# Two token-major projections joined into one 512 columns wide, in a two-layer hybrid decoder kernel

## The chip, the core and the metric

The kernel runs on one core of a Trainium2 chip. A core has TensorE (matrix products, PE in the profile, with its weight loads listed apart as PEld), VectorE (DVE), ScalarE (ACT), GpSimd (POOL) and a queue that only starts transfers (SP). Each of them works through its own list of instructions in order, and semaphores hold an instruction back until what it needs has been done elsewhere. The metric is the device time of one execution in microseconds (us), lower is better. Three runs of the kernel before took 1769.89, 1771.38 and 1771.6 us; their median is 1771.38.

## The reference

The computation is a decoder trunk of two equal layers on 512 tokens of width 1024. Cut to what matters here, a layer is:

```python
h = rms_norm(x, ln1)
u = h @ w_in                       # one projection; its columns are split among all branches
(fq, fk, fv, ff, gq, gk, gv, glr, gr, rq, rk, rv, rg, z, xbc, dt, gates) = split_cols(u, IN_SPLITS)
y_a = forgetting_attention(fq, fk, fv, ff + fox_bf, ...)      # softmax attention with decay
o_b = gla_chunked(gq, gk, gv, log_a)                          # gated linear attention
o_c = retention_chunked(rotary(rq), rotary(rk), rv, log_gamma)
o_d = ssd_chunked(...)                                        # state-space scan
x = x + (sum over the branches of sigmoid(gate_b) * (y_b @ w_up_b)) @ w_out
x = x + swiglu(rms_norm(x, ln2), w_ffn_in, w_ffn_out)
```

`fv` and `rv` are the values of the forgetting attention and of the retention: 512 tokens by 256 columns each.

## The kernel before, in words

**Products.** To keep float32 accuracy, every operand of a large product is split into a high and a low part in a reduced-precision format (`xh` and `xl` for the normed input, `wh` and `wl` for weights). One logical product is then three matrix instructions into the same PSUM bank, issued by `mm3` (line 164): high by high, low of the stationary side by high, high by low of the moving side. All of them go through line 162, so the profile gives nearly all of TensorE's work that one line, and the tiles tell the work apart. A name like `mm<-xh,wl` reads: result in an `mm` bank, moving operand `xh`, stationary operand `wl`.

**Weights.** All weights come as 300 slabs of eight 128 by 128 blocks, in the order in which `block` (line 236) asks for them. For each slab there is one transfer (`wr`), a cast on ACT to `wh` (line 176) and a subtraction on DVE to `wl` (line 177). Two slabs of raw weights and three of split weights fit in SBUF.

**Projections.** Most column groups of `w_in` are projected feature-major: the weight block is stationary, 512 tokens move, eight steps of the inner dimension give 24 instructions into one bank (`proj`). The first four of a layer run together step by step into four `mx` banks (`group`), since at the start weights and inputs are only arriving. The values are needed token-major: there the tokens are stationary (128 at a time, four groups `tb`) and the weight columns move. `tokmajor` (line 469) does this for `rv` and, later, for `fv`: 256 columns move, two groups of tokens share a bank, so one such projection uses two of the four `mm` banks. At its end ACT scales the results of `rv` by the norm (`v`), and for `fv` ACT writes a high part and DVE the low part of a split tile (lines 490 and 491).

**Order of the work.** The four mixers (`ssd`, `gla`, `ret`, `fox`) are chains of small products, exponentials and elementwise work. Each is a Python generator, and at each `yield` the function `drain` lets `pull` emit dense projections from the list `fill`, until their costs (the numbers that stand with them in the list, in us) add up to a budget, `PACE`. What a projection costs over the budget is owed and is taken from the next ones. So the costs in the list set which dense work stands between two steps of a chain. A scheduler then sets the final order of each engine's list, with its own model of time.

In `gla`, the steps that matter here are: cumulated gates by small float32 products (line 784) into two banks `mx`; from each bank an exponential on ACT (line 786), a product on POOL with the queries (line 787), a second exponential and a product on DVE with the keys (line 790), a copy and a subtraction on DVE (lines 793 and 796); then products of those queries and keys, the scores (line 811), after memsets on POOL of parts of the tiles that will take them (line 815).

Of the kernel before, what the change touches and what calls it, by code (L numbers as in the profile page):

```python
# [10 lines left out]
F32 = mybir.dt.float32  # L11
F32R = mybir.dt.float32r
I32 = mybir.dt.int32
AF = mybir.ActivationFunctionType
ALU = mybir.AluOpType
# [3 lines left out]
P = 128  # L19
S = 512  # L20
D = 1024
KD = D // P
NB = S // P
# [3 lines left out]
NH = 4  # L27
# [3 lines left out]
C_FQ, C_FK, C_FV, C_FF = 0, 256, 512, 768  # L31
C_GQ, C_GK, C_GV, C_GLR, C_GR = 772, 1028, 1284, 1540, 1556
C_RQ, C_RK, C_RV, C_RG = 1812, 2068, 2324, 2580
# [92 lines left out]
def trunk(ctx: ExitStack, tc: tile.TileContext, keys, xin, pos, wst, par, ext, cst, out):  # L126
    nc = tc.nc
    V, A, G, T = nc.vector, nc.scalar, nc.gpsimd, nc.tensor
# [5 lines left out]
    vp = ctx.enter_context(tc.tile_pool(name="vp", bufs=2))  # L134
# [7 lines left out]
    def nm(s):  # L142
        uid[0] += 1
        return f"{s}{uid[0]}"

    def TT(dtype=F32):
        return tp.tile([P, S], dtype, tag="t", name=nm("t"))

    def MM():
        return pm.tile([P, S], F32, tag="mm", name=nm("mm"))  # L150
# [10 lines left out]
    def mm(o, l, r, start, stop):  # L161
        T.matmul(o, lhsT=l, rhs=r, start=start, stop=stop, skip_group_check=True)  # L162

    def mm3(o, l, r, start, stop):
        (lh, ll), (rh, rl) = l, r
        mm(o, lh, rh, start, False)
        mm(o, ll, rh, False, False)
        mm(o, lh, rl, False, stop)

    def mm2(o, l, r, start, stop):  # L170
        pairs = [(a, r) for a in l] if isinstance(l, tuple) else [(l, b) for b in r]
# [19 lines left out]
    def act(out, in_, func, **kw):  # L191
        want = {AF.Ln: "natural_log_exp_and_others", AF.Exp: "natural_log_exp_and_others", AF.Silu: "silu_and_others", AF.Sin: "silu_and_others", AF.Sigmoid: "sigmoid_and_others"}.get(func)
        pre = None
        if want and want != seen["set"]:
            pre = A.preload_act_table_set(want)  # L195
            if seen["last"] is not None:
                order(pre, seen["last"])
            seen["set"] = want
            seen["pre"] = pre
        i = A.activation(out=out, in_=in_, func=func, **kw)  # L200
        if want:
            order(i, seen["pre"])
            seen["last"] = i
        return i
# [31 lines left out]
    def block(*key, width=1):  # L236
        n = len(keys)
        if n % SLAB == 0:
            ahead(n // SLAB + AHEAD)
            if n // SLAB:  # L240
                ready[n // SLAB - 1] = None
        for i in range(width):
            keys.append(key[:-1] + (key[-1] + i * P,))
        i = n % SLAB
        hi, lo = ready[n // SLAB]
        sl = slice(i * P, (i + width) * P)
        return hi[:, sl], lo[:, sl]
# [153 lines left out]
    def layer(l, n1):  # L401
# [4 lines left out]
        fill = []  # L406
# [59 lines left out]
                dst[i] = scaled(proj("w_in", l, c, n1, KD), scale)  # L466
            return TILE, go

        def tokmajor(dst, c, stacked=False):
            st = {}  # L470

            def go(half):
                def f():
                    if half == 0:
                        if not stacked:
                            dst.append(vp.tile([P, NB, 256], F32, tag="v", name=nm("v")))
                        st["ps"] = [MM(), MM()]
                    for k in range(4 * half, 4 * half + 4):
                        w = block("w_in", l, k, c, width=2)
                        for tb in range(NB):  # L480
                            ts = slice(tb * P, (tb + 1) * P)
                            o = st["ps"][tb // 2][:, (tb % 2) * 256:(tb % 2) * 256 + 256]
                            mm3(o, (n1.hi[:, k, ts], n1.lo[:, k, ts]), w, k == 0 and tb % 2 == 0, k == KD - 1)
                    if half:
                        for tb in range(NB):
                            v, rt = st["ps"][tb // 2][:, (tb % 2) * 256:(tb % 2) * 256 + 256], n1.rt[:, tb:tb + 1]
                            if stacked:
                                t = TT(F32R).rearrange("p (h s d) -> p h s d", h=NH, s=2)
                                v = v.rearrange("p (h d) -> p h d", h=NH)
                                act(out=t[:, :, 0], in_=v, func=AF.Copy, scale=rt)  # L490
                                V.scalar_tensor_tensor(out=t[:, :, 1], in0=v, scalar=rt, in1=t[:, :, 0].bitcast(F32), op0=ALU.mult, op1=ALU.subtract)
                                dst.append(t)
                            else:
                                act(out=dst[0][:, tb], in_=v, func=AF.Copy, scale=rt)
                return f
            return [(4.1, go(0)), (4.1, go(1))]

        if l == 0:
            rotary()
# [6 lines left out]
        for k in range(KD):  # L506
            w = wide(l, k)
# [629 lines left out]
        fill += silus([C_GR, C_GR + P, C_RG, C_RG + P])  # L1137
        fill += [keep(rq, j, C_RQ + P * j) for j in range(2)] + [keep(rk, j, C_RK + P * j) for j in range(2)]
        drain(ssd(), PACE[0])
        fill += tokmajor(rv, C_RV)  # L1140
        fill += gate_quad(3, 0) + mix(gate_quad(3, 1), up_of(3, 0))
        drain(gla(), PACE[1])
        fill += [keep(fq, j, C_FQ + P * j) for j in range(2)] + [keep(fk, j, C_FK + P * j) for j in range(2)]
        fill += [(0.0, fox_sums)] + tokmajor(fv, C_FV, True) + [(0.0, fox_rows)]
        fill += mix(gate_quad(1, 0), up_of(3, 1)) + mix(gate_quad(1, 1), up_of(1, 0))
        drain(ret(), PACE[2])
        fill += mix(gate_quad(2, 0), up_of(1, 1)) + mix(gate_quad(2, 1), up_of(2, 0)) + mix(gate_quad(0, 0), up_of(2, 1))
# [144 lines left out]
```

## Time and profile before

| | |
|---|---|
| median of three runs | 1771.38 us (1769.89 to 1771.6) |
| profiled execution, its own time | 1771.39 us |
| span of its instructions | 1769.7 us (1.7 us lie around it) |
| TensorE matmuls | busy 1760.0 us, 99% of the span, 8700 instructions |
| TensorE weight loads | busy 1463.6 us, 83%, 8700 instructions |
| VectorE, ScalarE, GpSimd | busy 1041.5, 684.8 and 230.3 us |
| mean granted TensorE clock | 0.999 |

Matmuls are pipelined: a record of one is longer than the distance to the next, so the distance between two starts is what an instruction costs on TensorE, and a busy share of 99% only says that there is hardly a stretch without any. Weight loads run beside the matmuls before them. In a row of the timeline, the first two columns are the start and the length in us, `x4` is the count that was merged into the row, and brackets tell how long the engine had been idle before it and what ended that. In a row of a group, the numbers behind the bar are the busy time in us, the mean length of one in ns and the idle time before them.

### The profile page before, as it was taken

The numbers are of one execution on the slowest core, as the hardware profiler recorded it, in microseconds if no ns is written. First come the engines' busy times: TensorE is split into PE (matmuls) and PEld (weight loads), VectorE is DVE, ScalarE is ACT, GpSimd is POOL, SyncE is SP. The second block draws the span as 40 slices with busy tenths as digits, with TensorE's granted clock in tenths as the row PEclk, the third lists the DMA queues.
The fourth block names the chain that finished last, engine by engine and source line by source line (L and its number), as shares of the span: only waits on it lengthen the run. The fifth ranks groups of instructions, "written<-read, shape, count | busy, mean of one in ns | idle before, by whom it ended". The sixth has DMA issues, their size and how long they took to land.

```text
span 1769.7 us, 21568 instructions
## 1 busy us (share of the span) xinstructions
PE 1760.0 (99%) x8700; PEld 1463.6 (83%) x8700; DVE 1041.5 (59%) x1427; ACT 684.8 (39%) x926; POOL 230.3 (13%) x210
## 2 busy tenths in 40 slices
PE   8999999999999999999999999999999999999999
PEld 7878888888888888888888788888888888888887
DVE  5866675777674443444447676867775644334442
ACT  5424543555443321223324254345554432223221
POOL 2032120022101110011000321201220111001100
PEclk9999999999999999999999999999999999999999
DMA  5322222222232222222323222222222323222222
GB/s 188 108 72 72 73 84 77 91 84 84 93 98 95 96 95 96 96 97 95 107 84 107 72 73 71 84 84 84 95 79 84 103 96 101 98 95 96 95 96 95
DMA packets 46036, 163.31 MB, mean 92 GB/s; under 512 B 5104, under 2 KB 5488, under 8 KB 45936
## 3 DMA queue, kind: packets, MB, share of 16 engines
q1 hardware_dynamic: 45072, 160.45, 27.5%
q10 hardware_dynamic: 864, 1.48, 0.3%
q8 instruction: 68, 1.11, 0.3%
q14 instruction: 32, 0.26, 0.1%
HBM read 159.81 MB, written 2.10 MB: 91 GB/s over the span
## 4 chain that ended last, share of the span: by engine, by line
PE 98%; ACT 0%; DVE 0%; DMA 0%; issue 0%; DVEq 0%; ACTq 0%
PE mm L162 83%; PE mx L162 14%; PE mx L1033 1%; DMA x<-in_x_dram 0%; PE mx L633 0%; DVE xl L355 0%; DVE t L367 0%; ACT xh L200 0%; ACT t L200 0%; PE mx L905 0%; PE mx L825 0%; DVE wl L177 0%; ACT wh L176 0%; ACT L195 0%; PE mx L621 0%
## 5 line engine op out<-in xcount | busy, mean ns | idle before, releaser
L176 ACT CAST wh<-wr 128x1024 fp32r<-128x1024 f32 (+1 forms) x300 | 313.1, 1045 | 737.8 <-PE mm L162 599.5
L162 PE MATMUL mm<-xh,wl 128*128 128x512 f32 x1504 | 589.2, 392 | 0.0
L162 PE MATMUL mm<-xh,wh 128*128 128x512 f32 x1504 | 589.1, 392 | 0.0
L162 PE MATMUL mm<-xl,wh 128*128 128x512 f32 x1504 | 588.1, 391 | 0.0
L177 DVE TENSOR_TENSOR wl<-wr,wh 128x1024 fp32r<-128x1024 f32 (+1 forms) x300 | 409.9, 1366 | 285.6 <-ACT wh L176 284.6
L162 PE MATMUL mm<-t,wh 128*128 128x512 f32 x1152 | 367.5, 390 | 0.0
L162 PEld LDWEIGHTS mm<-xh,wh 128*128 128x128 f32 x1504 | 282.5, 188 | 58.9 <-issue 1.3
L162 PEld LDWEIGHTS mm<-xl,wh 128*128 128x128 f32 x1504 | 282.5, 188 | 58.9 <-issue 1.3
L162 PEld LDWEIGHTS mm<-xh,wl 128*128 128x128 f32 x1504 | 282.6, 188 | 58.5 <-issue 1.1
L162 PEld LDWEIGHTS mm<-t,wh 128*128 128x128 f32 x1152 | 216.4, 188 | 44.7
L162 PE MATMUL mm<-t,wl 128*128 128x512 f32 x576 | 224.8, 390 | 0.0
L1178 POOL TENSOR_TENSOR t<-t,t 128x512 f32<-128x512 f32 x44 | 56.8, 1290 | 538.6 <-DVE t L1176 467.4
L162 PEld LDWEIGHTS mm<-t,wl 128*128 128x128 f32 x576 | 108.2, 188 | 22.0
L176 ACT CAST t<-t 128x512 fp32r<-128x512 f32 x112 | 68.7, 621 | 88.5 <-POOL t L1178 42.0
L177 DVE TENSOR_TENSOR t<-t,t 128x512 fp32r<-128x512 f32 x112 | 78.2, 704 | 29.6 <-ACT t L176 22.9
L1176 DVE TENSOR_TENSOR t<-mm,t 128x512 f32<-128x512 f32 x40 | 27.7, 691 | 115.0 <-PE mm L162 115.0
L200 ACT ACTIVATE t<-t 128x512 f32<-128x512 f32 x121 | 73.7, 628 | 24.2 <-DVE t L1175 14.5
L1126 POOL TENSOR_TENSOR t<-t,t 128x512 f32<-128x512 f32 x32 | 43.6, 1361 | 249.1 <-DVE t L1122 243.7
L162 PE MATMUL mx<-t,t 64*128 64x128 f32 (+6 forms) x576 | 63.8, 290 | 0.0
L1175 DVE TENSOR_TENSOR t<-mm,t 128x512 f32<-128x512 f32 x40 | 27.6, 691 | 61.1 <-PE mm L162 61.1
L162 PEld LDWEIGHTS mx<-t,t 128*128 128x128 f32 (+3 forms) x576 | 50.5, 165 | 14.2 <-issue 8.0
L162 PE MATMUL mx<-xh,wl 128*128 128x512 f32 x128 | 50.7, 400 | 3.0 <-DVE wl L177 3.0
(210 smaller groups left out, 1661.2 us busy)
## 6 DMA issues: line engine op xcount, KB each, us to landing
wr<-in_wst_dram SPq DMA_DIRECT2D x296, 512.0 KB, 3.3
out_dram<-x SPq DMA_DIRECT2D x8, 256.0 KB, 2.4
x<-in_x_dram SPq DMA_DIRECT2D x3, 512.0 KB, 6.3
wr<-in_wst_dram SPq DMA_DIRECT2D x4, 256.0 KB, 5.9
x<-in_x_dram SPq DMA_DIRECT2D x2, 256.0 KB, 5.4
cs<-in_cst_dram ACTq DMA_DIRECT2D x1, 462.0 KB, 5.9
pr<-in_par_dram ACTq DMA_DIRECT2D x2, 167.0 KB, 5.1
posi<-in_pos_dram ACTq DMA_DIRECT2D x1, 256.0 KB, 6.8
```

What stands on the lines that cost most here:

```text
L162: T.matmul(o, lhsT=l, rhs=r, start=start, stop=stop, skip_group_check=True)
L176: A.copy(out=hi, in_=src)
L177: V.tensor_tensor(out=lo, in0=src, in1=hi.bitcast(F32), op=ALU.subtract)
L200: i = A.activation(out=out, in_=in_, func=func, **kw)
L1033: T.transpose(ps[:, W:W + P], zs[qb][:, kb * P:(kb + 1) * P], ident)
L1126: (V if last else G).tensor_tensor(out=merged[d], in0=merged[d], in1=t, op=ALU.add)
L1175: V.tensor_tensor(out=a, in0=pg, in1=n2.r, op=ALU.mult)
L1176: V.tensor_tensor(out=u, in0=pu, in1=n2.r, op=ALU.mult)
L1178: G.tensor_tensor(out=a, in0=a, in1=u, op=ALU.mult)
```

## The change

`tokmajor` now does both projections at once: it asks for the blocks of `rv` and `fv` together (two blocks each), moves 512 columns, and gives each of the four groups of tokens a bank of its own, so that it takes all four `mm` banks. At its end it empties each bank three times: ACT for `rv`, ACT and DVE for `fv`. Its two halves stand in the list at a cost of 7.6 each, at the place where `rv` stood alone at 4.1 each (the fill of `gla`); the place of `fv` in the fill of `ret` is empty. In `mm3` the last two of the three products change places, so that the two which share the stationary high part follow each other. `block` learns to take a tuple of two columns.

```diff
     def mm3(o, l, r, start, stop):
         (lh, ll), (rh, rl) = l, r
         mm(o, lh, rh, start, False)
-        mm(o, ll, rh, False, False)
-        mm(o, lh, rl, False, stop)
+        mm(o, lh, rl, False, False)
+        mm(o, ll, rh, False, stop)
...
         for i in range(width):
-            keys.append(key[:-1] + (key[-1] + i * P,))
+            c = key[-1][i // 2] + i % 2 * P if isinstance(key[-1], tuple) else key[-1] + i * P
+            keys.append(key[:-1] + (c,))
...
-        def tokmajor(dst, c, stacked=False):
-            st = {}
+        def tokmajor():
+            st = []
 
             def go(half):
                 def f():
                     if half == 0:
-                        if not stacked:
-                            dst.append(vp.tile([P, NB, 256], F32, tag="v", name=nm("v")))
-                        st["ps"] = [MM(), MM()]
+                        rv.append(vp.tile([P, NB, 256], F32, tag="v", name=nm("v")))
+                        st.extend(MM() for _ in range(NB))
                     for k in range(4 * half, 4 * half + 4):
-                        w = block("w_in", l, k, c, width=2)
+                        w = block("w_in", l, k, (C_RV, C_FV), width=4)
                         for tb in range(NB):
                             ts = slice(tb * P, (tb + 1) * P)
-                            o = st["ps"][tb // 2][:, (tb % 2) * 256:(tb % 2) * 256 + 256]
-                            mm3(o, (n1.hi[:, k, ts], n1.lo[:, k, ts]), w, k == 0 and tb % 2 == 0, k == KD - 1)
+                            mm3(st[tb], (n1.hi[:, k, ts], n1.lo[:, k, ts]), w, k == 0, k == KD - 1)
                     if half:
                         for tb in range(NB):
-                            v, rt = st["ps"][tb // 2][:, (tb % 2) * 256:(tb % 2) * 256 + 256], n1.rt[:, tb:tb + 1]
-                            if stacked:
-                                t = TT(F32R).rearrange("p (h s d) -> p h s d", h=NH, s=2)
-                                v = v.rearrange("p (h d) -> p h d", h=NH)
-                                act(out=t[:, :, 0], in_=v, func=AF.Copy, scale=rt)
-                                V.scalar_tensor_tensor(out=t[:, :, 1], in0=v, scalar=rt, in1=t[:, :, 0].bitcast(F32), op0=ALU.mult, op1=ALU.subtract)
-                                dst.append(t)
-                            else:
-                                act(out=dst[0][:, tb], in_=v, func=AF.Copy, scale=rt)
+                            rt = n1.rt[:, tb:tb + 1]
+                            t = TT(F32R).rearrange("p (h s d) -> p h s d", h=NH, s=2)
+                            v = st[tb][:, 256:].rearrange("p (h d) -> p h d", h=NH)
+                            act(out=rv[0][:, tb], in_=st[tb][:, :256], func=AF.Copy, scale=rt)
+                            act(out=t[:, :, 0], in_=v, func=AF.Copy, scale=rt)
+                            V.scalar_tensor_tensor(out=t[:, :, 1], in0=v, scalar=rt, in1=t[:, :, 0].bitcast(F32), op0=ALU.mult, op1=ALU.subtract)
+                            fv.append(t)
                 return f
-            return [(4.1, go(0)), (4.1, go(1))]
+            return [(7.6, go(0)), (7.6, go(1))]
...
-        fill += tokmajor(rv, C_RV)
+        fill += tokmajor()
...
-        fill += [(0.0, fox_sums)] + tokmajor(fv, C_FV, True) + [(0.0, fox_rows)]
+        fill += [(0.0, fox_sums), (0.0, fox_rows)]
```

What the built lists show at three places follows; rows stand as the lists have them, and numbers in the names tell buffers apart. Lines of the changed kernel lie three lower in `gla` than those of the profile (784 for 787 and so on).

**The start, third slab of weights.** TensorE, the first `group` of the first layer (`mx12` to `mx15` are its four banks, `wh16` and `wl17` the two parts of the third slab). Before:

```order
L162 MATMUL mx12_149<-xh6_119,wh16_177 128x512 [waits Activation_49]
L162 MATMUL mx13_150<-xh6_119,wh16_177 128x512
L162 MATMUL mx14_151<-xh6_119,wh16_177 128x512
L162 MATMUL mx15_152<-xh6_119,wh16_177 128x512
L162 MATMUL mx12_149<-xh6_119,wl17_178 128x512 [waits DVE_49]
L162 MATMUL mx12_149<-xl7_120,wh16_177 128x512
```

And now:

```order
L162 MATMUL mx12_149<-xh6_119,wh16_177 128x512 [waits Activation_49]
L162 MATMUL mx12_149<-xl7_120,wh16_177 128x512 [waits DVE_49]
L162 MATMUL mx13_150<-xh6_119,wh16_177 128x512
L162 MATMUL mx13_150<-xl7_120,wh16_177 128x512
L162 MATMUL mx14_151<-xh6_119,wh16_177 128x512
L162 MATMUL mx14_151<-xl7_120,wh16_177 128x512
L162 MATMUL mx15_152<-xh6_119,wh16_177 128x512
L162 MATMUL mx15_152<-xl7_120,wh16_177 128x512
L162 MATMUL mx12_149<-xh6_119,wl17_178 128x512 [waits DVE_49]
```

Before, four products stand ahead of the first that needs the low part of the weights; now eight do.

**The end of the joint projection, the start of `gla`.** TensorE, first layer. `mx286` and `mx291` are the two banks of cumulated gates, `mm313` is a dense projection. Before, ahead of the scores:

```order
L162 MATMUL mx286_1627<-cr_99,t276_1504 128x128 [waits DVE_49]
L162 MATMUL mx286_1627<-cr_99,t276_1504 128x128
L162 MATMUL mx291_1645<-cr_99,t276_1504 128x128 x2
L162 MATMUL mm313_1768<-xh6_119,wh307_1719 128x512
L162 MATMUL mm313_1768<-xh6_119,wl308_1720 128x512
```

Some 30 dense products follow in that list before the first of the scores. Now the two banks are `mx288` and `mx293`, `mm281` is the fourth bank of the joint projection, the scores go to `mx308` and `mx309`, and `mm313`, the next dense projection, takes over the bank of the first group of tokens:

```order
L162 MATMUL mx293_1595<-cr_99,t276_1504 128x128 x2
L162 MATMUL mm281_1516<-wl300_1616,xh6_119 128x512
L162 MATMUL mm281_1516<-wh299_1615,xl7_120 128x512
L162 MATMUL mx308_1689<-t125_824,t290_1585 128x128 [waits DVE_49,PE_49,Pool_49]
L162 MATMUL mx309_1690<-t125_824,t290_1585 128x128 [waits PE_49]
L162 MATMUL mx308_1689<-t125_824,t290_1585 128x128
L162 MATMUL mx309_1690<-t125_824,t290_1585 128x128
L162 MATMUL mx308_1689<-t125_824,t290_1585 128x128
L162 MATMUL mx309_1690<-t125_824,t290_1585 128x128
L162 MATMUL mx308_1689<-t125_824,t290_1585 128x128
L162 MATMUL mx309_1690<-t125_824,t290_1585 128x128
L162 MATMUL mm313_1710<-xh6_119,wh302_1645 128x512 [waits DVE_49]
```

Two dense products are left between the cumulated gates and the scores. The four products into `mx288` and two more into `mx293` stand directly ahead of this piece. The second layer has the same sequence.

**DVE and POOL at that place, now.** On DVE, `t290` and `t295` are the products with the keys, `t304` is the low part of `fv` of the first group of tokens, read from the bank that `mm313` waits for:

```order
L787 TENSOR_TENSOR t290_1585<-t152_941,t290_1585 128x512 [waits Activation_49]
L790 COPY bl291_1588<-mx288_1577 128x8 [waits PE_49]
L793 TENSOR_TENSOR t289_1582<-bl291_1588,mx288_1577 128x512 [waits DVE_49,Pool_49]
L787 TENSOR_TENSOR t295_1603<-t166_1000,t295_1603 128x512 [waits Activation_49]
L790 COPY bl296_1606<-mx293_1595 128x8 [waits PE_49]
L490 SCALAR_TENSOR_TENSOR t304_1673<-mm278_1513,rt40_317,t304_1673 128x4x64 [waits Activation_49]
```

Before, no reading of a value bank stood among these. On POOL, all four memsets now stand between the two products with the queries, where one stood before:

```order
L784 TENSOR_TENSOR t125_824<-t125_824,t289_1582 128x512 [waits Activation_49]
L812 MEMSET t310_1699 64x4x64 [waits DVE_49]
L812 MEMSET t311_1704 64x4x64 [waits DVE_49]
L812 MEMSET t319_1752 64x4x64 [waits DVE_49]
L812 MEMSET t320_1757 64x4x64 [waits DVE_49]
L784 TENSOR_TENSOR t142_892<-t142_892,t294_1600 128x512 [waits Activation_49]
```

The other three memsets had been issued ahead of the first of these products.

## The prediction

> **What bounds the kernel now.** I read the page first: the busy times and the chain that ended last.
>
> ```profile
> PE 1760.0 (99%) x8700; PEld 1463.6 (83%) x8700; DVE 1041.5 (59%) x1427; ACT 684.8 (39%) x926; POOL 230.3 (13%) x210
> PE 98%; ACT 0%; DVE 0%; DMA 0%; issue 0%; DVEq 0%; ACTq 0%
> ```
>
> TensorE carries the chain from end to end, so the time is the number of its instructions times their distance, plus the few stretches in which it waits. The distance comes from the timeline: ten feature-major products, then fifteen of the projection of `rv`.
>
> ```profile
> 360.68 0.39 PE L162 MATMUL mm<-xl,wh 128*128 128x512 f32 x1
> ...
> 362.95 0.39 PE L162 MATMUL mm<-t,wh 128*128 128x512 f32 x1
> ...
> 171.19 0.28 PE L162 MATMUL mm<-wl,xh 128*128 128x256 f32 x1
> ...
> 172.99 0.28 PE L162 MATMUL mm<-wl,xh 128*128 128x256 f32 x1
> ```
>
> 512 columns take (362.95 - 360.68) / 10 = 0.227 us and 256 columns (172.99 - 171.19) / 15 = 0.120 us. Twice 0.120 less 0.227 leaves 0.013 us: each instruction costs that much whatever its width.
>
> Where TensorE waits, the first 30 us show it: the first `group`, at its third slab of weights.
>
> ```profile
> 20.25 1.07 PE L162 MATMUL mx<-xh,wh 128*128 128x512 f32 x4
> 23.92 0.80 PE L162 MATMUL mx<-xh,wl 128*128 128x512 f32 x1 [2.60 <-DVE wl L177]
> 24.51 0.63 PE L162 MATMUL mx<-xl,wh 128*128 128x512 f32 x1
> ...
> 27.07 0.52 PE L162 MATMUL mx<-xl,wh 128*128 128x512 f32 x1
> 27.43 0.40 PE L162 MATMUL mx<-xh,wh 128*128 128x512 f32 x1
> ...
> 30.15 1.07 PE L162 MATMUL mx<-xh,wh 128*128 128x512 f32 x4
> ```
>
> The same place in windows of 3.4 us; the columns are the busy time of PE, PEld, DVE, ACT and POOL, each with its count, then the granted clock, the DMA share and GB/s.
>
> ```profile
> 20.50:23.92 3.42, 0.82 (x4) 0.35 (x3) 3.42 (x4) 1.05 (x1) 3.30 (x5) 1.00 0.00 0
> 23.92:27.33 3.41, 3.41 (x8) 2.73 (x9) 2.70 (x3) 0.80 (x2) 0.41 (x1) 0.50 0.60 183
> ```
>
> After a window in which TensorE was busy for 0.82 of 3.42 us, it got half the clock for the next 3.41 us, and eight products from 23.92 to 27.43 cost 0.43 us each instead of 0.227. The waits of TensorE and a window over the rest show that nothing of the kind comes later:
>
> ```profile
> PE mx L162 <- DVE wl L177: 3.0, 2, 2.6
> 40.00:1760.00 1720.00, 1720.00 (x8535) 1431.38 (x8534) 1017.64 (x1399) 662.21 (x892) 219.36 (x196) 1.00 0.27 90
> ```
>
> From 40 to 1760 us it is busy without a gap and at full clock.
>
> **The change part by part.** *Half as many instructions, each twice as wide.*
>
> ```profile
> L162 PE MATMUL mm<-wh,xh 128*128 128x256 f32 x128 | 36.4, 284 | 0.0
> L162 PE MATMUL mm<-wh,xl 128*128 128x256 f32 x128 | 36.2, 283 | 0.0
> L162 PE MATMUL mm<-wl,xh 128*128 128x256 f32 x128 | 36.2, 283 | 0.0
> ```
>
> These are 384 instructions on the path, 384 x 0.120 = 46.1 us. They become 192 at 0.227, 43.6 us: **-2.5 us**. The evacuations (eight of `rv`, eight pairs of `fv`) stay the same in number and width.
>
> *The order within mm3.* Over the whole list, 85 neighbours shared a stationary operand before, and 2407 do now: 2322 new pairs. Such a pair exists in the trace, a sum over the partitions whose high and low parts both meet the constant ones (`cr`):
>
> ```profile
> 298.64 0.41 PEld L162 LDWEIGHTS mx<-t,cr 128*128 128x128 f32 x2
> 298.87 0.62 PE L162 MATMUL mx<-t,cr 128*128 128x512 f32 x2
> 299.33 0.40 PE L162 MATMUL mm<-t,wh 128*128 128x512 f32 x1
> ```
>
> Two loads for two products, and (299.33 - 298.87) / 2 = 0.230 us each, against 0.227 where the operand changes. The load is part of each product, it is hidden either way, and its repetition saves nothing. I take **0**; 0.003 us either way, the size of that difference, would be 7 us over 2322 pairs, and I keep that as a bound of low weight. The Trainium skill ("TensorE: Matmul & The Clock Gate", Part 2) says that loading apart from computing lets one load serve many products; the trace shows that this program doesn't do so. What it would give is the third rival.
>
> *The start.* In the third slab, eight products instead of four now stand ahead of the wait for `wl` (the first pair of lists above). The wait itself ends where it did, since DVE comes to that subtraction without a pause and without TensorE:
>
> ```profile
> 19.07 2.44 DVE L355 SCALAR_TENSOR_TENSOR xl<-x,pr,xh 128x512 fp32r<-128x512 f32 x2
> 21.43 1.09 DVE L367 TENSOR_TENSOR t<-t,t 128x512 f32<-128x512 f32 x1
> 22.44 1.42 DVE L177 TENSOR_TENSOR wl<-wr,wh 128x1024 fp32r<-128x1024 f32 x1
> ```
>
> From 23.92 on four products of this step are left instead of eight. If the clock still halves: 4 x 0.43 to 25.64, four of the next twelve to 27.36, eight at 0.227 to 29.18, where 30.15 stands above: **-1.0 us**. If it stays full (TensorE would be busy for about 1.5 us of that window instead of 0.82): 16 x 0.227 to 27.55, -2.6 us. I take -1.0 and keep both ends.
>
> *The start of gla, in each layer.* Here the change adds two waits. Before, a long stretch of dense work lay between the cumulated gates and the scores; now, by the list above, two products do. The chain in between, from the trace of before:
>
> ```profile
> 194.95 1.05 PE L162 MATMUL mx<-cr,t 128*128 128x128 f32 x8
> 195.76 0.48 PE L162 MATMUL mm<-xh,wh 128*128 128x512 f32 x1
> 195.59 2.07 ACT L200 ACTIVATE t<-mx 128x512 f32<-128x512 f32 x4 [0.97 <-PE mx L162]
> 196.27 1.29 POOL L787 TENSOR_TENSOR t<-t,t 128x512 f32<-128x512 f32 x1 [20.71 <-ACT t L200]
> 197.51 0.31 POOL L815 MEMSET t<- 64x256 f32 x1
> 197.78 1.49 POOL L787 TENSOR_TENSOR t<-t,t 128x512 f32<-128x512 f32 x1
> 196.71 1.40 DVE L790 TENSOR_TENSOR t<-t,t 128x512 f32<-128x512 f32 x1 [0.84 <-ACT t L200]
> 198.03 0.15 DVE L793 COPY bl<-mx 128x8 f32<-128x8 f32 x1
> 198.11 1.70 DVE L790 TENSOR_TENSOR t<-t,t 128x512 f32<-128x512 f32 x1
> 199.81 1.27 DVE L796 TENSOR_TENSOR t<-bl,mx 128x512 f32<-128x512 f32 x2
> ```
>
> Count from u, the start of ACT's first exponential (195.59). The DVE product with the keys ends at u + 2.52, stretched: both times DVE ends 0.55 us after POOL's product does (198.11 after 197.56, 199.81 after 199.27). TensorE gets there earlier. Small products start every 0.11 us; ACT starts 0.31 after the last one into the first bank (195.59 against about 195.28). Behind that one now stand eight records and two dense products, 0.11 + 0.88 + 0.45 = 1.44, so TensorE is at the scores at about u + 1.15 and waits until u + 2.55: **1.4 us**.
>
> The second wait is for a bank. The eight scores take 1 us (16 of them took 1.99 before):
>
> ```profile
> 202.53 2.06 PE L162 MATMUL mx<-t,t 64*128 64x128 f32 x32
> 204.52 0.50 PE L162 MATMUL mm<-xl,wh 128*128 128x512 f32 x1
> L491 DVE SCALAR_TENSOR_TENSOR t<-mm,rt,t 128x256 fp32r<-128x256 f32 x8 | 3.7, 481 | 6.8 <-ACT t L200 6.7
> ```
>
> So TensorE is at `mm313` at u + 3.55, and that waits until DVE has read the low part of `fv` from the first bank. Ahead of this read DVE has a copy (0.08 to the next start), a subtraction (0.60), the second product with the keys and another copy. The second product could start at u + 2.44 + 0.08 + 0.60 = u + 3.12. POOL starts its second product after four memsets instead of one, 1.92 + 4 x 0.27 = u + 3.0, narrowly ahead. Then DVE ends 0.55 us after POOL's 1.49 us, at u + 5.05; copy and read (0.48) free the bank at u + 5.6: **2.1 us** of waiting. ACT's part (one more scaling of that bank, behind its four exponentials) is done before. With DVE narrowly ahead, its product takes what it takes between other tiles, 0.70 us:
>
> ```profile
> L177 DVE TENSOR_TENSOR t<-t,t 128x512 fp32r<-128x512 f32 x112 | 78.2, 704 | 29.6 <-ACT t L176 22.9
> ```
>
> The bank is then free at u + 4.4, and the wait is 0.8 us.
>
> Two layers: 2 x (1.4 + 2.1) = **+7.0 us**, or +4.4. Below I count no gain: nothing else could fill these waits, since TensorE's list is fixed.
>
> *The rest.* The fill of `ret` is shorter by the `fv` projection, so later dense work moves up and the end of `fox` has less left. In its list a projection there waits for a bank behind a few DVE operations of 0.5 to 0.7 us; I take 0, up to 0.7 per layer.
>
> Sum against the profiled execution: 1771.39 - 2.5 - 1.0 + 7.0 = **1774.9 us**. Its own time is the median of the runs shown to 0.01 us. About 0.2% (3.5 us) is what a measurement here can tell from no change; the forecast is +3.5 us, at that edge, and I call it the upper end of "same".
>
> **The rivals.**
>
> *DVE first.* The race by 0.1 us goes the other way in both layers: 1774.9 - 2.6 = 1772.3. For it: POOL's memsets might go faster if they are not held up. Against: the 0.27 us between 197.51 and 197.78 is their measured distance.
>
> *The clock halves after the waits: slower.* From the start of the first wait to the end of the second lie 4.4 us with 1 us of small products and little else; a window of 3.41 us can hold 2.4 us of idle time, 1.0 of 3.41 busy, where 0.82 of 3.42 was enough at the start. Each such drop costs half a window, 1.7 us: one in each layer gives 1778.3, one alone 1776.6. It decides by how the windows lie, which the list does not tell. The Trainium skill (the same page, "Why this matters for your kernels") warns of gaps above some 3 us only; by that neither of these waits would drop the clock. The trace differs: a wait of 2.60 us did.
>
> *Shared loads.* If neighbours with one stationary operand skipped the second load, and with it the fixed 0.013 us, 2322 pairs would save up to 30 us: about 1745. The pair above and equal counts of loads and products (8700 each) speak against it; a fraction of it is within the 7 us named.
>
> *The waits are hidden.* If other work of the list covers them after all, 1771.4 - 3.5 = 1767.9, or 1766.3 with the clock kept at the start. Against: the list leaves two products.
>
> **How the numbers follow.** The forecast gets 0.35, DVE first 0.20, the clock 0.27, shared loads 0.06, hidden waits 0.12. Slower by over 0.2%, above 1774.9: the clock and, since the forecast sits on the edge, half of its case: 0.27 + 0.17 = 0.44. Faster, below 1767.8: shared loads and most of the hidden waits, 0.16. The rest, 0.40, is within 0.2%. The range runs from 1768.5 (most of the hidden waits and the shared loads fall out) to 1779 (both layers with a slower clock and some more at the end of `fox`); what lies outside is about 0.2.
>
> **What the changed profile would show.** 192 products of `wh` and `wl` by 512 columns at 0.227 us, and none by 256. Pairs of one `wh` with two loads at 0.227 to 0.230. At the start four products, not eight, after the wait for `wl`. In each layer two idle stretches of TensorE, ended by DVE or POOL at the scores and by DVE at the next dense projection, 1.4 and 2.1 us, with POOL's second product just ahead of DVE's; windows of clock 0.50 there if the second rival holds. The prediction is wrong if the loads fall below the products, if these stretches are missing, or if a wait appears elsewhere.

## The result, and the profile after

| | time, us (median) | runs | lowest to highest | against before |
|---|---|---|---|---|
| before | 1771.21 | 9 | 1769.89 to 1771.6 | |
| after | 1775.37 | 9 | 1773.52 to 1777.1 | 1.0024 [1.0014, 1.0034] |

The change costs 4.2 us, 0.24%. The forecast was 1774.9 us, +3.5 us, at the edge of the 0.2% that a measurement can tell; the result lies just beyond it. The profiled execution took 1775.69 us, against 1771.39 before: 4.3 us to explain.

The nine times come in steps of about 1.7 us: 1773.52 and 1773.75 (mean granted clock 1.000), five from 1775.14 to 1775.69 (0.998 or 0.999), 1776.47 (0.998) and 1777.1 (0.996).

The page has 192 products and 192 loads fewer than before, and DVE and ACT now stand in the chain that ended last:

```profile
span 1773.9 us, 21179 instructions
...
PE 1759.1 (99%) x8508; PEld 1453.6 (82%) x8508; DVE 1049.6 (59%) x1427; ACT 683.6 (39%) x926; POOL 233.2 (13%) x210
...
PE 98%; DVE 1%; ACT 1%; DMA 0%; issue 0%; DVEq 0%; ACTq 0%
```

The waits of TensorE (total, how many, the longest) show two kinds that before did not have, once in each layer: the scores wait for DVE (`bl`, line 790), and the next dense projection waits for DVE's reading of a value bank (`t`, line 490).

```profile
PE mm L162 <- DVE t L490: 2.9, 2, 1.5
PE mx L162 <- ACT wh L176: 2.7, 1, 2.7
PE mx L162 <- DVE bl L790: 2.6, 2, 1.3
PE mx L162 <- DVE wl L177: 1.6, 1, 1.6
```

The start of `gla` in the first layer, in order of time:

```profile
191.29 2.06 ACT L200 ACTIVATE t<-mx 128x512 f32<-128x512 f32 x4 [0.64 <-PE mx L162]
191.97 1.27 POOL L784 TENSOR_TENSOR t<-t,t 128x512 f32<-128x512 f32 x1 [22.57 <-ACT t L200]
192.22 0.40 PE L162 MATMUL mm<-wh,xl 128*128 128x512 f32 x1
192.41 1.38 DVE L787 TENSOR_TENSOR t<-t,t 128x512 f32<-128x512 f32 x1 [4.68 <-ACT t L200]
...
193.93 1.16 PE L162 MATMUL mx<-t,t 64*128 64x128 f32 x16 [1.32 <-DVE bl L790]
...
194.21 1.26 POOL L784 TENSOR_TENSOR t<-t,t 128x512 f32<-128x512 f32 x1
...
194.57 1.45 DVE L787 TENSOR_TENSOR t<-t,t 128x512 f32<-128x512 f32 x1
...
196.02 1.65 DVE L490 SCALAR_TENSOR_TENSOR t<-mm,rt,t 128x256 fp32r<-128x256 f32 x4
...
196.54 0.80 PE L162 MATMUL mm<-xh,wh 128*128 128x512 f32 x1 [1.45 <-DVE t L490]
...
197.14 0.63 PE L162 MATMUL mm<-xl,wh 128*128 128x512 f32 x1
197.56 0.63 PE L162 MATMUL mm<-xh,wl 128*128 128x512 f32 x1
```

The last product of the joint projection starts at 192.22; TensorE then stands idle 1.32 us, does one set of scores, and stands idle another 1.45 us. As forecast, POOL's second product (194.21) is just ahead of DVE's (194.57), and DVE's ends at 196.02, 0.55 us after POOL's (195.47). From start to start, beyond what the product ahead costs, the two stretches are 1.49 and 1.66 us, to 0.01 us the same in both layers: 6.3 us in all.

The clock in windows over both layers and at the start (columns as in the prediction). In this trace all changes of the granted clock lie whole multiples of 3.413 us apart, and the windows are laid on that grid:

```profile
8.32:11.73 3.41, 3.30 (x8) 2.63 (x9) 2.20 (x4) 3.38 (x7) 0.00 (x0) 0.50 1.04 403
...
192.64:196.05 3.41, 1.16 (x16) 1.00 (x16) 3.31 (x6) 3.41 (x10) 2.83 (x6) 1.00 0.02 5
196.05:199.47 3.42, 2.93 (x7) 2.35 (x8) 3.39 (x8) 2.41 (x8) 1.75 (x2) 0.50 0.01 2
1069.87:1073.28 3.41, 2.17 (x18) 1.73 (x16) 1.45 (x2) 2.77 (x7) 1.89 (x4) 1.00 0.02 6
1073.28:1076.69 3.41, 1.88 (x19) 1.63 (x20) 3.31 (x8) 3.41 (x10) 2.07 (x4) 1.00 0.00 0
```

In the first layer both waits fall into one window, in which TensorE is busy for 1.16 us, and the next 3.42 us run at half the clock (products 0.43 us apart: 197.14, 197.56), which costs 1.7 us. In the second layer an edge of the grid (1073.28) parts the same two waits, the windows have 2.17 and 1.88 us of work, and the clock stays full. The first row is another stretch at half clock, at the start of the kernel.

### The profile page after: what moved, and what is told of

It reads as the page before. It is cut to its first block, busy times and chain, and to the rows that moved or that the text cites. A ratio compares the mean times of both kernels' runs of the same rounds, so it can differ in the third digit from the quotient of the medians.

```text
span 1773.9 us, 21179 instructions
## 1 busy us (share of the span) xinstructions
PE 1759.1 (99%) x8508; PEld 1453.6 (82%) x8508; DVE 1049.6 (59%) x1427; ACT 683.6 (39%) x926; POOL 233.2 (13%) x210
## 4 chain that ended last, share of the span: by engine, by line
PE 98%; DVE 1%; ACT 1%; DMA 0%; issue 0%; DVEq 0%; ACTq 0%
PE mm L162 83%; PE mx L162 14%; PE mx L1030 1%; DVE t L787 0%; DMA x<-in_x_dram 0%; ACT t L200 0%; PE mx L630 0%; DVE xl L356 0%; DVE t L368 0%; ACT xh L200 0%; PE mx L902 0%; PE mx L822 0%; DVE wl L177 0%; ACT wh L176 0%; ACT L195 0%
## 5 line engine op out<-in xcount | busy, mean ns | idle before, releaser
L177 DVE TENSOR_TENSOR wl<-wr,wh 128x1024 fp32r<-128x1024 f32 (+1 forms) x300 | 414.1, 1382 | 257.4 <-ACT wh L176 255.6
L162 PE MATMUL mm<-t,wh 128*128 128x512 f32 x1152 | 356.0, 390 | 0.0
L1105 DVE TENSOR_TENSOR g<-mm,t 128x512 f32<-128x512 f32 x64 | 43.8, 686 | 32.7 <-PE mm L162 32.1
```

What stands on the lines that cost most here:

```text
L177: V.tensor_tensor(out=lo, in0=src, in1=hi.bitcast(F32), op=ALU.subtract)
L1105: V.tensor_tensor(out=st["t"][:, i], in0=ps, in1=n1.r, op=ALU.mult)
```

## The experiments

**The theory.** Of the 4.3 us, the two waits per layer make +6.3 and the half-clock stretch +1.7; the fewer instructions give 2.5 back and the start about 2 (some 0.6 us more are spread over the rest). TensorE waits because its list has nothing left that could run: the joint projection holds all four `mm` banks, and until one is read no dense product can start. **Rivals:** the order within `mm3` itself costs something or saves loads; the move of `fv` away from `ret` takes cover from there; the waits come from the costs in the list and not from the banks.

The experiments ran on three chips; each ratio is against runs of the kernel before on the same chip, whose median stands beside it.

| label | time, us | runs | before there, us | against before |
|---|---|---|---|---|
| order_only | 1768.81 | 11 | 1771.44 | 0.9985 [0.9976, 0.9994] |
| sep_both | 1769.77 | 11 | 1771.44 | 0.9992 [0.9983, 1.0001] |
| joint_only | 1780.61 | 5 | 1771.44 | 1.0053 [1.0041, 1.0066] |
| cost41 | 1784.57 | 5 | 1771.44 | 1.0073 [1.0060, 1.0086] |
| groups_first | 1775.19 | 8 | 1771.48 | 1.0028 [1.0017, 1.0038] |
| memset_early | 1775.23 | 11 | 1770.14 | 1.0024 [1.0015, 1.0033] |
| shift_gate | 1766.97 | 11 | 1770.14 | 0.9977 [0.9968, 0.9986] |
| shift_old | 1770.56 | 11 | 1770.14 | 0.9998 [0.9989, 1.0007] |

**order_only: the order within mm3 alone.** The kernel before, with one edit:

```diff
         mm(o, lh, rh, start, False)
-        mm(o, ll, rh, False, False)
-        mm(o, lh, rl, False, stop)
+        mm(o, lh, rl, False, False)
+        mm(o, ll, rh, False, stop)
```

> The kernel before with only the order within mm3 changed: both projections stay 256 wide and where they were. The theory (two waits per layer at the start of gla make the time, less the fewer instructions and a shorter start): only the start gains, 1.0 to 2.6 us, so 1768.6 to 1770.2 us against 1771.2, products 0.227 us apart as before, as many weight loads as products (8700). Rival, the order costs: if 2322 new neighbours with the same stationary operand each lose 0.002 us or so, 1773 us or more. Rival, shared loads: fewer loads than products and a gain of up to 30 us, about 1745.

Measured 1768.81 us, 2.6 us below the before of the same chip (1771.44). The page and the wait for the third slab's low part:

```profile
PE 1758.8 (100%) x8700; PEld 1463.0 (83%) x8700; DVE 1049.7 (59%) x1427; ACT 685.1 (39%) x926; POOL 235.2 (13%) x210
...
24.19 1.21 PE L162 MATMUL mx<-xh,wl 128*128 128x512 f32 x4 [1.74 <-DVE wl L177]
```

Loads still equal products, so no load is shared, and the order costs nothing. The gain is the start: a wait of 1.74 us where before had 2.60, and no half clock after it (the next products follow at 0.23 us: 25.24, 25.48, 25.70). That the gain is 2.6 us and not 1.0 means that the full-clock end of the forecast's two was the right one. Both rivals on the order fall.

**sep_both: both projections at the start of gla, but not joined.** The changed kernel with the old `tokmajor` put back, 256 columns, two banks each, and four pieces at 3.8 in the list:

```diff
-        fill += tokmajor()
+        fill += tokmajor(rv, C_RV) + tokmajor(fv, C_FV, True)
```

> Both projections one behind the other at the start of gla, each 256 wide in two banks as before the change, four pieces at 3.8 in the list; new order within mm3. By its list 9 narrow and 26 wide dense products stand between the last cumulated gates and the scores. The theory: no wait there, the start gains as in the changed kernel, the narrow products cost their 2.5 us: 1768.6 to 1770.2 us. Rival, the move of fv to the start of gla is what costs (its place in ret was cover that is now missing there): waits appear in ret or fox, 1773 us or more.

Measured 1769.77 us, within the theory's bounds. TensorE has no wait at `gla`, and its waits end with the start of the kernel:

```profile
PE mx L162 <- ACT wh L176: 2.3, 3, 1.7
PE mx L162 <- DVE wl L177: 1.8, 1, 1.8
PE mm L162 <- POOL t L286: 1.4, 1, 1.4
```

So moving `fv` brings no wait, and the same sum of costs (15.2 a layer) at the same place makes none. The move is not free, though: order_only, with the same order and nothing moved, took 0.96 us less on the same chip (1768.53 to 1769.02 us against 1769.61 to 1769.9), and no single wait accounts for that. What differs from the changed kernel is the join, with its width and its four banks, but also the size of the pieces (four of 3.8 instead of two of 7.6), on which it depends when the budget draws them.

**joint_only: the join with the old order within mm3.** The diff of order_only, the other way round, on the changed kernel.

> The changed kernel with the old order within mm3, so the joint projection alone. The theory: the waits at the start of gla stay (1.5 and 1.7 us in each layer, and a stretch at half clock in one of them or none), the gain at the start is lost: 1776 to 1778.5 us, 1 to 2.6 us above the changed kernel; TensorE waits 2.6 us for the low part of the third slab, as before the change. Rival, the order within mm3 is what costs: the slowdown goes, 1769 us or below.

Measured 1780.61 us: slower, as the theory has it, but 2 us beyond its bounds. The second layer has the waits of the changed kernel (1.49 and 1.66 us from start to start). The first layer does not:

```profile
194.27 0.48 PE L162 MATMUL mm<-wl,xh 128*128 128x512 f32 x1
...
194.84 1.90 DVE L177 TENSOR_TENSOR wl<-wr,wh 128x1024 fp32r<-128x1024 f32 x1 [5.21 <-ACT t L200]
...
196.66 1.77 DVE L787 TENSOR_TENSOR t<-t,t 128x512 f32<-128x512 f32 x1
...
198.58 2.08 PE L162 MATMUL mx<-t,t 64*128 64x128 f32 x16 [3.83 <-DVE bl L790]
```

There a conversion of weights on DVE (line 177) stands ahead of the product with the keys, and the first wait is 3.83 instead of 1.32 us. No second wait follows, but the granted clock is 0.50 from 198.06 to 204.89 us, for two windows of the grid instead of one. Against the profiled execution of the changed kernel (1775.69 us) this one (1781.64 us) is 1.9 us longer at the start, 2.3 us at this place and about 2 us over the rest; why the rest is longer stays open. An uncovered chain is as long as whatever an engine's list happens to put into it.

**cost41: the same join, cheaper in the list.**

```diff
-            return [(7.6, go(0)), (7.6, go(1))]
+            return [(4.1, go(0)), (4.1, go(1))]
```

> The changed kernel with the two halves of the joint projection at 4.1 in the list instead of 7.6, so that two more gate projections are drawn in at the start of gla; now 30 dense products stand between the cumulated gates and the scores. The theory: both waits go, and what is left are the fewer instructions (2.5 us) and the start (1 to 2.6 us): 1766 to 1768 us, faster than both kernels; by up to 0.6 us more if the first of these dense products has to wait for the bank of the first group of tokens. Rival, taking all four banks is what costs: the wait for that bank moves to the first dense product behind the gates and stays about 1.7 us in each layer, 1770 us.

Measured 1784.57 us, the slowest of all, some 16 us beyond the theory's bounds. At the start of `gla` both waits are gone (30 dense products cover the chain, as its list says). They come back in `fox`:

```profile
PE mx L162 <- ACT t L176: 5.3, 2, 2.7
PE mm L162 <- DVE g L1105: 3.1, 4, 1.1
...
400.00:500.00 100.00, 95.25 (x449) 77.89 (x448) 66.81 (x110) 47.69 (x67) 14.55 (x19) 1.00 0.24 79
```

From 400 to 500 us TensorE is idle for 4.75 us, and as much in the second layer. At 8.2 instead of 15.2 a layer the budget drew 7 us more dense work into `gla` and `ret`, and `fox`, whose cover it had been, ran short. Thirteen distances over 0.48 us, in `fox` and ahead of it, make 12.1 us more than 0.227 us each. In the second layer the longest of these waits is also followed by 3.42 us at half clock (granted 0.50 from 1311.91 us). The rival on the bank falls too: no wait for the bank of the first tokens is seen. With the cheaper cost the second half of the join comes ahead of the gates, and its readings with it: DVE reads the first bank at 189.08 us, and ACT's first exponential starts at 192.01.

**groups_first: the bank's last product earlier.** The second half, group of tokens by group of tokens:

```diff
-                    for k in range(4 * half, 4 * half + 4):
-                        w = block("w_in", l, k, (C_RV, C_FV), width=4)
-                        for tb in range(NB):
-                            ts = slice(tb * P, (tb + 1) * P)
-                            mm3(st[tb], (n1.hi[:, k, ts], n1.lo[:, k, ts]), w, k == 0, k == KD - 1)
+                    ks = range(4 * half, 4 * half + 4)
+                    w = [block("w_in", l, k, (C_RV, C_FV), width=4) for k in ks]
+                    for tb in range(NB):
+                        ts = slice(tb * P, (tb + 1) * P)
+                        for k in ks:
+                            mm3(st[tb], (n1.hi[:, k, ts], n1.lo[:, k, ts]), w[k % 4], k == 0, k == KD - 1)
```

> The changed kernel with the second half of the joint projection written group of tokens by group of tokens, so that the bank of the first group gets its last product 15 products (3.4 us) or more ahead of the end instead of 9 (2.0 us). The theory (what holds the bank is the place of its last reading in DVE's list, behind both products with the keys, whenever the products end): the same two waits, 1.5 and 1.7 us in each layer, 1773.5 to 1777 us like the changed kernel. Rival, the bank is free late because its last product is late: the second wait goes, 2 x 1.7 us less, 1770 to 1773 us.

Measured 1775.19 us, the changed kernel's time, though two of the eight runs (1779.68 and 1779.79 us) lie above the theory's 1777. In the first layer ACT scales the `rv` half of the first bank 4.8 us ahead of the start of the joint projection's last product, instead of 3.4 us, and then touches that bank for 5.8 us no more:

```profile
187.25 0.47 ACT L200 ACTIVATE v<-mm,rt 128x256 f32<-128x256 f32 x1 [0.31 <-PE mm L162]
...
191.08 2.06 ACT L200 ACTIVATE t<-mx 128x512 f32<-128x512 f32 x4 [1.09 <-PE mx L162]
...
193.01 1.23 ACT L200 ACTIVATE t<-mm,rt 128x256 fp32r<-128x256 f32 x3
...
196.34 0.79 PE L162 MATMUL mm<-xh,wh 128*128 128x512 f32 x1 [1.45 <-DVE t L491]
```

In ACT's list the copies of `fv` stand behind the four exponentials of the gates (191.08), in DVE's the reading stands behind both products with the keys. The bank waits for its place in these lists, not for its products. (In the second layer the list differs a little; there the waits are 1.09 and 0.52 us, and a half set of scores fills the gap.)

**memset_early: what holds DVE's second product.** The four memsets on POOL (line 812), and the tiles they write, are issued ahead of the cumulated gates:

```diff
+            at = {}
+            for j in range(2):
+                for half in range(2):
+                    at[j, half] = TT()
+                    G.memset(chunked(at[j, half])[:64, :, 64:], 0.0)
             yield 2
...
-                    t = TT()
+                    t = at[j, half]
                     tv, pv = chunked(t), chunked(ps)
-                    G.memset(tv[:64, :, 64:], 0.0)
```

> The changed kernel with the four memsets on POOL issued ahead of the cumulated gates, so that POOL's second product with the queries follows its first at once. The theory (the second wait of each layer is DVE's second product with the keys, held until 0.55 us after POOL's): POOL is through 1.0 us earlier, DVE's product takes about 0.7 us, the bank is read about 0.7 us earlier: the second wait 0.9 instead of 1.7 us, 2 x 0.75 us less in all, 1773.0 to 1774.8 us. Rival, POOL's two products back to back keep DVE from its first product as well: the first wait grows from 1.5 to about 2.7 us, and the time is 1775.5 to 1777.5 us.

Measured 1775.23 us, no gain; the lowest runs show none either (1773.96 us, and 1773.52 for the changed kernel). The wait itself shrank as the theory has it, but the list changed as well:

```profile
191.27 2.95 POOL L789 TENSOR_TENSOR t<-t,t 128x512 f32<-128x512 f32 x2 [21.57 <-ACT t L200]
...
193.23 1.16 PE L162 MATMUL mx<-t,t 64*128 64x128 f32 x16 [1.32 <-DVE bl L795]
...
193.87 0.89 DVE L792 TENSOR_TENSOR t<-t,t 128x512 f32<-128x512 f32 x1
...
194.91 1.13 PE L162 MATMUL mx<-t,t 64*128 64x128 f32 x8 [0.52 <-DVE bl L795]
195.97 0.50 PE L162 MATMUL mm<-xh,wh 128*128 128x512 f32 x1
```

DVE's second product takes 0.89 instead of 1.45 us (it ends at 194.76, 0.54 us after POOL's), the first wait stays at 1.32 us, and no wait is left at the dense projection. But half of the next scores now stand here, and TensorE waits 0.52 us for those. They are of one half of the 128 rows only, and eight records take 0.9 us; the row at 193.23 has sixteen, of both halves in turn, in the same time. The other half follows later, again alone. From start to start the two layers save 2 x (1.66 - 0.72) = 1.9 us of waiting and lose 2 x 0.9 us to scores that no longer run in pairs. The profiled execution (1777.08 us) is one of the slowest: in its second layer the clock is halved from 1073.38 to 1080.21 us, for two windows, in its first not at all. The rival (a longer first wait) falls; the theory's saving was there and was spent elsewhere.

**shift_gate: the reading ahead of the gates, dense work behind them.** The changed kernel with the costs at 7.6; one pull is given earlier and taken back later, so that the sum over `gla` stays:

```diff
-            yield 2
+            yield 3
             qd, ki, ke, dcs = [], [], [], []
...
                     at[j, half] = t
-                yield
+                yield j
             kt = []
```

> The changed kernel with the costs at 7.6, but one pull's worth of budget taken from the step after the first scores and given to the step before the cumulated gates; the sum over gla stays. By its list the second half of the joint projection and its evacuations are now issued ahead of the gates, and 30 dense products stand between the last of the gates and the scores. The theory (TensorE had nothing to do there because every bank was still unread): both waits go, nothing is missing later, 1765.5 to 1767.5 us, 8 to 10 us below the changed kernel and about 4.5 below before. Rival, the cover is only moved: waits of the same size come up later in gla, in ret or in fox as with the lower cost, 1771 us or more.

Measured 1766.97 us, 11 runs between 1766.84 and 1767.2: within the theory's bounds and 8.4 us below the changed kernel. It is faster than before by 0.23% [0.14, 0.32], that is 3.2 us on this chip, where the theory had some 4.5. Its waits:

```profile
PE mx L162 <- ACT wh L176: 2.1, 3, 1.6
PE mx L162 <- DVE wl L177: 1.8, 1, 1.8
PE mm L162 <- POOL t L286: 1.4, 1, 1.4
```

The start of `gla` in it, ACT, DVE and TensorE:

```profile
188.30 0.47 ACT L200 ACTIVATE v<-mm,rt 128x256 f32<-128x256 f32 x1 [2.35 <-PE mm L162]
...
189.17 0.48 DVE L490 SCALAR_TENSOR_TENSOR t<-mm,rt,t 128x256 fp32r<-128x256 f32 x1 [1.96 <-ACT t L200]
...
191.84 0.48 PE L162 MATMUL mm<-xh,wh 128*128 128x512 f32 x1
...
196.84 0.15 DVE L790 COPY bl<-mx 128x8 f32<-128x8 f32 x1
...
198.83 2.06 PE L162 MATMUL mx<-t,t 64*128 64x128 f32 x32
...
400.00:500.00 100.00, 100.00 (x472) 83.26 (x471) 69.92 (x104) 45.39 (x62) 15.35 (x15) 1.00 0.29 95
```

The first bank is read by 189.65, so the next projection starts at 191.84 right behind the gates; the chain to both products with the keys is even longer than before (to 196.91, that is 4.8 us behind the start of ACT's first exponential at 192.10, against 4.2), but the scores stand at 198.83. `fox` (400 to 500) has no idle time: the cover was not taken from there. Beside sep_both, with the same order and no waits either, it is 2.8 us faster: the join, at 2.5 us by the count of instructions (the two ran on different chips, where the lowest times of before are 0.2 us apart).

**shift_old: the same without the new order.** The two edits of shift_gate on joint_only.

> The same shift, with the old order within mm3: the joint projection without its waits and without the better start. The theory: only the fewer instructions are left, 192 products of 512 columns at 0.227 us for 384 of 256 at 0.120, 2.5 us: 1768 to 1769.2 us; 1 to 2.6 us above the shift with the new order. Rival, a new order is needed for the join to pay: no difference from before, 1771 us.

Measured 1770.56 us, 1.4 us above the theory's bounds and 3.6 above shift_gate. By the medians this is the rival's outcome: no difference from before can be told (0.9998 [0.9989, 1.0007]). At its lowest step (1769.22 to 1769.37, four runs) it is 0.6 us below the lowest of before on that chip (1769.7 to 1770.14, 14 runs), not 2.5. Its profile shows a part of the rest:

```profile
PE mx L162 <- DVE wl L177: 2.4, 1, 2.4
...
PE mm L162 <- DVE wl L177: 0.3, 2, 0.2
```

Two small waits in `fox` for the low part of a new slab cost 0.31 us each from start to start; in feature-major projections the old order asks for that part as the second product, the new one as the third. About 1.2 us more is spread over many distances. Some 0.9 us of this kind stand in sep_both as well, against order_only, so most of it goes with the new place of `fv`; the remainder stays open.

## Why the forecast was nearly right

By its own steps:

- **Fewer instructions, -2.5 us: right.** The products of the joint projection follow at 0.227 us; between these two rows lie 66 of them, (189.52 - 174.56) / 66 = 0.2267:

```profile
174.56 0.39 PE L162 MATMUL mm<-wl,xh 128*128 128x512 f32 x1
...
189.52 0.39 PE L162 MATMUL mm<-wl,xh 128*128 128x512 f32 x1
```

  192 x 0.227 against 384 x 0.120 is -2.5, and shift_gate against sep_both is -2.8.
- **Order within mm3, 0: right,** with order_only. Part 2 of the Trainium skill's "TensorE: Matmul & The Clock Gate" says that one load can serve many products; here 8508 products have 8508 loads, with 2407 neighbours sharing an operand, and the rule brings nothing.
- **The start, -1.0 us: too little.** The wait for `wl` was 1.57 us and the clock stayed full, the forecast's other end (-2.6): TensorE was busy for 1.85 us of that window (21.97 to 25.39), where the forecast had reckoned about 1.5. Adding up, over the first 40 us, all that lies between starts beyond 0.013 us and 0.107 us per 256 columns gives 11.8 us before, 9.9 after (-1.8) and 9.6 in order_only. After loses the difference to a longer first wait for `wh` (2.66 us): its first product with weights starts at 8.43 us instead of 7.82, and in each of the ten profiles the wait for the third slab ends 16.10 to 16.12 us behind the start of that product. This holds with a half-clock stretch between the two (8.32 to 11.73 us in after) and without one (shift_gate), so that stretch cost nothing.
- **The first wait, 1.4 us: right.** 1.32 us idle, 1.49 from start to start.
- **The second wait, 2.1 us: right in kind, too long.** POOL was first, and DVE ended 0.55 us after it, as forecast. But POOL's second product took 1.26 us and not the 1.49 taken over from before, so the dense product starts 5.25 us after ACT's first exponential (196.54 - 191.29) and not 5.6, and the scores ahead of it end 0.05 us later than reckoned: 1.66 us from start to start. With the first wait that is 6.3 us in the two layers instead of 7.0.
- **The clock after the waits (a rival at +1.7 us): it came in part.** One stretch in the profiled execution, in the first layer, and none in the second; the places of the windows decided it, as the forecast has it. The steps of the nine times fit 0, 1 or 2 windows at half clock behind these waits, one in the median; only one of the nine was profiled, so that reading is argued.
- **The rest, 0:** by the same adding up, outside the start, the waits and the slow stretch, +0.6 us. The forecast had up to 0.7 per layer for the place that `fv` left in `ret`; sep_both, which moves `fv` without a join, has 0.9 us of this kind against order_only.

So -2.5 - 1.8 + 6.3 + 1.7 + 0.6 = +4.3 us. The forecast's +3.5 came from -2.5 - 1.0 + 7.0: the start was mis-sized by 0.8 and the waits by 0.7 the same way, and the clock, which the likeliest case left out, made up for both, with the rest on top. The waits and their causes were forecast; that the number came so close is partly luck. The two runs with a mean granted clock of 1.000 took 1773.52 and 1773.75 us, below the forecast.

What the forecast did not give was the reason for the empty list. Three runs bear on it: without the join there is no wait (sep_both), an earlier last product does not help (groups_first), and an earlier reading, with dense work behind the gates, does (shift_gate). That the second wait is for the reading of the bank, wherever its products end, is shown by the traces of after and groups_first. That the full banks also make the first wait is argued: sep_both has smaller pieces too, and shift_gate and cost41 move the readings and the dense work in one step, so no run parts the banks from the budget. Without these waits the change is a gain, of 0.23% in shift_gate, of which order_only alone has 0.15%.

## What to carry to other kernels

A joined projection that takes every bank of a pool can be a barrier: here the next dense projection could not start until the first bank had been read, so the evacuations should stand ahead of the next chain in the lists of the engines that do them. Where an idle stretch of the bound engine is to be filled, move the cover with its budget kept in sum: cheaper costs filled this gap and opened a larger one 200 us later. And count a chain that has just lost its cover at more than its own length, since whatever an engine's list puts into it (here a conversion of weights, +2.5 us) is now on the path.

## What the runs showed of the hardware

- **It is the work in a fixed window of 3.41 us that decides whether the clock is halved, not the length of one wait.** In each of the ten profiles all changes of the granted clock lie whole multiples of 3.413 us apart. On this grid, from the first clock record on, 19 windows at full clock had TensorE busy for 1.57 us or less, and half the clock followed each time; no window with 1.67 us or more was followed by it. The nearest two cases are from memset_early, with the window behind it at half clock, and order_only, whose next window ran at 1.00:

```profile
1069.97:1073.38 3.41, 1.57 (x19) 1.28 (x19) 3.31 (x7) 3.41 (x8) 2.46 (x2) 1.00 0.00 0
1073.38:1076.79 3.41, 3.41 (x13) 2.80 (x13) 3.38 (x7) 3.24 (x9) 2.11 (x2) 0.50 0.00 0
...
21.27:24.68 3.41, 1.67 (x8) 1.08 (x7) 3.41 (x4) 0.13 (x1) 3.21 (x4) 1.00 0.00 0
```

  The grid lies differently in each profile (an edge 1.49 us behind the start of the span in after, 0.02 us in before), and that is the chance in it: two idle stretches of 1.3 and 1.45 us in one window halved the clock, the same two on either side of an edge did not. The half clock lasted one window in after, two in joint_only and memset_early at this place; why stays open. The kernels without these waits and without a long one at the start scatter far less: 0.4 us for shift_gate, 0.5 us for order_only, against 3.6 us for after and 6.4 us for groups_first. The Trainium skill ("TensorE: Matmul & The Clock Gate", "Why this matters for your kernels") warns of gaps above about 3 us; these runs show drops after gaps of half that.
- **A granted clock of 1.00 near the start can mean that there is no record.** In order_only the products from 8.66 to 10.80 us follow at 0.43 us, while a window over them shows 1.00; the first clock record of that trace stands at 11.03 us.
- **Products on 64 rows run in pairs.** Sixteen records that alternate between the two halves of the rows take the time of eight that use one half (0.9 us each in memset_early).
- **DVE behind POOL.** A product of two SBUF tiles on DVE that meets POOL's ended 0.54 or 0.55 us after POOL's in the changed kernel (both products), in joint_only (POOL's second product, DVE's first) and in memset_early (the second ones). The Trainium skill ("SBUF — State Buffer", "SBUF: two separate sides") calls the ports that the two share an exclusive lock for a whole instruction; the trace agrees in that DVE's product is held, though the 0.55 us that remain are less than the 0.68 us that the same product takes alone (joint_only, at 198.44).
